# Taking PEER's gate groups of four tokens two at a time

## The chip, the cores and the metric

The kernel runs on one core of a Trainium2 chip. The metric is device time in microseconds (us) of one execution, lower is better. The kernel before takes 1953.21 us, the median of three runs (1952.89 to 1954.54).

## What is computed

Two layers of a decoder trunk on 256 tokens of width 1024. Each layer is a mixer (attention or a matrix memory) followed by PEER, a retrieval of experts; the change is in PEER. There are 128 x 128 experts. For each token and each of 8 heads the 16 best experts are found, with a softmax gate each. Then, with `u` and `v` two tables of 16384 rows:

```
act = gelu(einsum('td,thkd->thk', xb, u[ib])) * gate     # 128 chosen experts of a token
out = einsum('thk,thkd->td', act, v[ib])
```

The kernel does not gather rows. It computes gelu(u . x) for all experts, 128 tiles of 128 experts, and multiplies it by a gate matrix that is zero except at the chosen experts. For one token that gate matrix, 128 x 128, is a product of two one-hot matrices: one marks the first half of each chosen expert's number, the other marks the second half and carries the gate.

## The kernel before, in words

In one PEER stage three things run beside each other.

**The u tiles** (`h_tile`, L964). For each of the 128 tiles, SyncE loads 512 KB of `u` into `raw`. ScalarE rounds it to `hi` (L155), and VectorE writes the difference `lo` (L158). `raw`, `hi` and `lo` have three buffers each, so `hi` of a tile can be written once TensorE is through with the tile three before it. TensorE then does the products. Three tiles of four are wide: eight products of 512 columns with `hi` (L976) and eight of 256 with `lo` (L980). The fourth is narrow: 24 products of 256 columns (L181 to L183, `lo` in L183). Both come to 6144 columns. ScalarE copies half of a wide tile's result to `hs` (L984), VectorE adds the other half (L985), and gelu goes to the big array A, half by half: tokens whose gate is already in A are multiplied (ScalarE L989, VectorE L990), the others are written (ScalarE L992).

**The one-hots** (`gate_onehots`, L1101), for a group of four tokens. `oi` is made on ScalarE (four squares L1108, one relu L1109) for five groups of eight, and on VectorE (L1111) for the other three. `oj` (one buffer, L1116) and `og` (L1118) are made on VectorE. `oi` and `og` have two buffers each.

**The gate products** (`gate_group`, L1122). Eight products of 128 columns (L1131), two for each token, fill one of the two `ps_g` banks. They are then merged into A: VectorE multiplies where gelu is already there (L1139), ScalarE copies where it is not (L1141).

There are 64 groups in a layer. After an even number of u tiles the loop takes as many groups as a straight line up to tile 120 asks for. Every engine's queue is in order. A scheduler places the instructions of the whole program in these queues, by its own estimate of when their operands are there, so the order in a queue is not just that of the code. When all tiles are done, the v products (L927 to L929) begin.

Groups are counted from 0 in each layer below, and [8, 9] is the pair of groups 8 and 9.

Of the kernel before, what the change touches and what calls it, by code (L numbers as in the profile page):

```python
# [23 lines left out]
T = 256  # L24
# [11 lines left out]
G_TOK = 4  # L36
# [38 lines left out]
class Prog:  # L75
# [749 lines left out]
    def peer_body(self, layer, side, st):  # L825
# [4 lines left out]
        oh = st.enter_context(tc.tile_pool(name=f"oh{layer}", bufs=2, reuse_waits="tile"))  # L830
        hp = self.hp
        a0 = st.enter_context(tc.tile_pool(name=f"a0{layer}", bufs=1, reuse_waits="tile"))
        tabs = {"i": tab.tile([P, T], F32, name="it"), "j": tab.tile([P, T], F16, name="jt"),
                "g": tab.tile([P, 2, T], F16, name="gt")}
# [33 lines left out]
        A, i = [A0], 0  # L868
# [13 lines left out]
        a1p = tc.tile_pool(name=f"a1{layer}", bufs=1, reuse_waits="tile")  # L882
        A.append(a1p.__enter__().tile([P, 32, T, 2], F32, name="A1"))
        i_start, done = i, 0
        ohs = self.gate_onehots(oh, tabs, 0)
        while i < NEXP:
            self.h_tile(u[i], h, A, i, done, h2 if i % MERGE_OF[0] < MERGE_OF[1] else None)
            i += 1
            while done < T and i % 2 == 0 and (i == NEXP or done < T * (i - i_start) / (I_STOP - i_start)):
                nxt = self.gate_onehots(oh, tabs, done + G_TOK) if done + G_TOK < T else None  # L890
                self.gate_group(ohs, A, done, i)
                ohs = nxt
                done += G_TOK
            yield
        acc = [self.psum("acc") for _ in range(4)]
        acts = hp.tile([P, 2, 2, 4, T], F32, tag="x", name="act")
# [2 lines left out]
        for n, e in enumerate(order):  # L899
# [19 lines left out]
            if n < NEXP - 3 or n == NEXP - 1:  # L919
                if n == NEXP - 1:  # L920
                    y = [late.tile([P, D], F32, tag="raw", name="y", bufs=LATE_RING) for _ in range(TT)]
                for q in range(4):
                    half, tt = q // 2, q % 2
                    c, t = slice(512 * half, 512 * half + 512), slice(tt * P, (tt + 1) * P)
# [321 lines left out]
```

## Time and profile before

| | before |
|---|---|
| time, median of three runs | 1953.21 us |
| profiled execution | 1958.02 us |
| its span, first to last instruction | 1956.2 us |
| TensorE busy with products | 1895.7 us, 97% |
| VectorE busy | 1524.4 us, 78% |
| ScalarE busy | 1164.1 us, 60% |
| gate products | 73.1 us, 1024 products |
| mean granted TensorE clock | 0.987 |

Busy time is that of the engine as a whole; overlapping instructions count once. A row of the timeline gives an instruction's start and how long it took. Since an instruction on ScalarE or VectorE begins before the one ahead of it is fully written, the step from one start to the next is a little shorter than the duration, and it is the step that a queue pays.

### The profile page before, as it was taken

The numbers are of one execution on the slowest core, as the hardware profiler recorded it, in microseconds if no ns is written. First come the engines' busy times: TensorE is split into PE (matmuls) and PEld (weight loads), VectorE is DVE, ScalarE is ACT, GpSimd is POOL, SyncE is SP. The second block draws the span as 40 slices with busy tenths as digits, with TensorE's granted clock in tenths as the row PEclk, the third lists the DMA queues.
The fourth block names the chain that finished last, engine by engine and source line by source line (L and its number), as shares of the span: only waits on it lengthen the run. The fifth ranks groups of instructions, "written<-read, shape, count | busy, mean of one in ns | idle before, by whom it ended". The sixth has DMA issues, their size and how long they took to land.

```text
span 1956.2 us, 31712 instructions
## 1 busy us (share of the span) xinstructions
PE 1895.7 (97%) x11733; PEld 1666.4 (85%) x11733; DVE 1524.4 (78%) x3183; ACT 1164.1 (60%) x2249; POOL 40.5 (2%) x37
## 2 busy tenths in 40 slices
PE   4988999999999999999999999999999999999999
PEld 4877999989999788888877799999999988888887
DVE  8886999789998656688568889988899965556655
ACT  4664555688876544444446654568888754444443
POOL 0010000000000000000001200000000000000000
PEclk9999999999999999999989999999999999999999
DMA  8872355555555677898447343554555556669760
GB/s 326 291 255 66 122 171 189 170 164 162 170 159 177 196 216 222 301 366 294 147 150 248 119 146 117 184 183 157 168 164 167 165 172 194 194 199 358 226 197 22
DMA packets 103979, 376.24 MB, mean 192 GB/s; under 512 B 11536, under 2 KB 12944, under 8 KB 103696
## 3 DMA queue, kind: packets, MB, share of 16 engines
q1 hardware_dynamic: 103824, 374.22, 57.7%
q8 instruction: 92, 1.51, 0.3%
q14 instruction: 63, 0.52, 0.1%
HBM read 373.12 MB, written 1.05 MB: 191 GB/s over the span
## 4 chain that ended last, share of the span: by engine, by line
PE 84%; DVE 7%; issue 4%; ACT 2%; DMA 1%; POOL 1%; POOLq 0%; DVEq 0%; ACTq 0%
PE ps_h L976 13%; PE ps_acc L928 12%; PE ps_acc L929 12%; PE ps_acc L927 12%; PE ps_h L181 7%; PE ps_h L183 7%; PE ps_h L182 7%; PE ps_h L980 6%; PE ps_g L1131 3%; DVE lo L158 2%; DVE raw L248 2%; PE ps_acc L999 1%; DMA raw<-in_ev_qk_dram 1%; POOL qr L258 1%; ACT hi L155 1%
## 5 line engine op out<-in xcount | busy, mean ns | idle before, releaser
L155 ACT CAST hi<-raw 128x1024 fp32r<-128x1024 f32 x613 | 645.5, 1054 | 585.2 <-PE ps_acc L928 309.8
L158 DVE TENSOR_TENSOR lo<-raw,hi 128x1024 fp32r<-128x1024 f32 x613 | 747.9, 1221 | 303.1 <-ACT hi L155 296.0
L927 PE MATMUL ps_acc<-hi,act 128*128 128x512 f32 x1024 | 398.2, 390 | 4.4 <-ACT act L908 4.4
L928 PE MATMUL ps_acc<-hi,act 128*128 128x512 f32 x1024 | 400.5, 391 | 0.3 <-DVE act L909 0.2
L929 PE MATMUL ps_acc<-lo,act 128*128 128x512 f32 x1024 | 400.5, 391 | 0.0
L976 PE MATMUL ps_h<-h,hi 128*128 128x512 f32 x1088 | 391.1, 400 | 0.0
L181 PE MATMUL ps_h<-h,hi 128*128 128x256 f32 x1216 | 349.9, 288 | 6.9 <-ACT h L465 3.4
L183 PE MATMUL ps_h<-h,lo 128*128 128x256 f32 x1216 | 345.9, 285 | 0.5 <-DVE lo L158 0.4
L182 PE MATMUL ps_h<-h,hi 128*128 128x256 f32 x1216 | 345.4, 284 | 0.8 <-DVE h L467 0.8
L980 PE MATMUL ps_h<-h,lo 128*128 128x256 f32 x1088 | 281.4, 279 | 0.0
L181 PEld LDWEIGHTS ps_h<-h,hi 128*128 128x128 f32 x1216 | 233.9, 193 | 9.2 <-ACT h L465 4.5
L182 PEld LDWEIGHTS ps_h<-h,hi 128*128 128x128 f32 x1216 | 234.1, 193 | 3.5 <-DVE h L467 1.3
L183 PEld LDWEIGHTS ps_h<-h,lo 128*128 128x128 f32 x1216 | 233.9, 192 | 1.9 <-DVE lo L158 1.2
L976 PEld LDWEIGHTS ps_h<-h,hi 128*128 128x128 f32 x1088 | 201.0, 188 | 35.3
L927 PEld LDWEIGHTS ps_acc<-hi,act 128*128 128x128 f32 x1024 | 192.4, 188 | 44.8 <-ACT act L908 4.8
L928 PEld LDWEIGHTS ps_acc<-hi,act 128*128 128x128 f32 x1024 | 193.1, 189 | 41.2 <-DVE act L909 1.2
L929 PEld LDWEIGHTS ps_acc<-lo,act 128*128 128x128 f32 x1024 | 193.2, 189 | 40.5 <-DVE lo L158 0.7
L980 PEld LDWEIGHTS ps_h<-h,lo 128*128 128x128 f32 x1088 | 205.0, 188 | 8.5 <-DVE lo L158 0.5
L248 DVE CUSTOM_DVE_ANT_0 raw<-raw,crow,small 128x1024 f32<-128x1024 f32 x96 | 122.5, 1279 | 22.0 <-DMA raw<-in_ada_w_dram 21.9
L1108 ACT ACTIVATE oi<-iota,it 128x128 f16<-128x128 f16 x320 | 107.9, 402 | 0.0
L1118 DVE TENSOR_TENSOR og<-oj,gt 128x1024 f16<-128x1024 f16 x128 | 87.6, 684 | 3.5 <-PE ps_g L1131 2.8
L984 ACT COPY hs<-ps_h 128x256 f32<-128x256 f32 x136 | 51.1, 376 | 58.0 <-PE ps_h L976 57.8
(318 smaller groups left out, 2240.8 us busy)
## 6 DMA issues: line engine op xcount, KB each, us to landing
raw<-in_uT_dram SPq DMA_DIRECT2D x256, 512.0 KB, 3.6
raw<-in_v_dram SPq DMA_DIRECT2D x256, 512.0 KB, 4.4
raw<-in_ada_w_dram SPq DMA_DIRECT2D x96, 512.0 KB, 5.2
raw<-in_wq_dram SPq DMA_DIRECT2D x32, 512.0 KB, 4.8
raw<-in_od_qk_dram SPq DMA_DIRECT2D x16, 512.0 KB, 5.2
raw<-in_ev_in_dram SPq DMA_DIRECT2D x13, 512.0 KB, 5.4
raw<-in_ev_v_dram SPq DMA_DIRECT2D x8, 512.0 KB, 4.5
raw<-in_ev_qk_dram SPq DMA_DIRECT2D x8, 512.0 KB, 5.2
```

Of the source, the lines that this page charges most:

```text
L155: nc.scalar.copy(hi, raw)
L158: self.last_lo = nc.vector.tensor_tensor(out=lo, in0=raw, in1=hi.bitcast(F32), op=ALU.subtract)
L181: nc.tensor.matmul(ps, lhsT=whi[:, s], rhs=ahi[:, kd, :], start=kd == kds[0], stop=False)
L182: nc.tensor.matmul(ps, lhsT=whi[:, s], rhs=alo[:, kd, :], start=False, stop=False)
L183: nc.tensor.matmul(ps, lhsT=wlo[:, s], rhs=ahi[:, kd, :], start=False, stop=kd == kds[-1])
L248: nc.vector.tensor_tensor_reduce(w, w, self.crow, 1.0, self.small[:, ab:ab + 1], ALU.mult, ALU.add, m)
L927: nc.tensor.matmul(acc[q], lhsT=xhi, rhs=vhi[:, c], start=m == 0, stop=False)
L928: nc.tensor.matmul(acc[q], lhsT=xlo, rhs=vhi[:, c], start=False, stop=False)
L929: nc.tensor.matmul(acc[q], lhsT=xhi, rhs=vlo[:, c], start=False, stop=m == NEXP - 1)
L976: wide = lambda: nc.tensor.matmul(ps, lhsT=whi[:, s], rhs=both[:, kd].rearrange("p a t -> p (a t)"), start=kd == 0, stop=kd == KD - 1)
L980: nc.tensor.matmul(ps[:, :T], lhsT=wlo[:, s], rhs=both[:, kd, 0], start=False, stop=False)
L1108: nc.scalar.activation(oi[:, k, :], self.iota, AF.Square, scale=-1.0, bias=tabs["i"][:, t0 + k:t0 + k + 1])
```

## The change

```diff
-        ohs = self.gate_onehots(oh, tabs, 0)
+        pair = lambda t0: [(t, self.gate_onehots(oh, tabs, t)) for t in (t0, t0 + G_TOK)]
+        ohs = pair(0)
         while i < NEXP:
             self.h_tile(u[i], h, A, i, done, h2 if i % MERGE_OF[0] < MERGE_OF[1] else None)
             i += 1
             while done < T and i % 2 == 0 and (i == NEXP or done < T * (i - i_start) / (I_STOP - i_start)):
-                nxt = self.gate_onehots(oh, tabs, done + G_TOK) if done + G_TOK < T else None
-                self.gate_group(ohs, A, done, i)
-                ohs = nxt
-                done += G_TOK
+                for t0, o in ohs:
+                    self.gate_group(o, A, t0, i)
+                done += 2 * G_TOK
+                if done < T:
+                    ohs = pair(done)
             yield
```

Before, the one-hots of the next group were written into the second buffer ahead of the products of this group. Now both buffers hold a pair, both groups are multiplied, and then both buffers are refilled. Lines below the edit are two higher in the changed kernel (L1118 is `og` before, L1120 after).

On TensorE the 128 groups of both layers stand in 84 unbroken runs before (22 of two groups and 20 of one in each layer) and in 74 after: 27 whole pairs in each layer, and five pairs that the scheduler cut in two, with products of a u tile between the parts. Three places in the other queues follow.

VectorE, around groups 8 to 11 of the first layer, before (`lo` is the difference of a u tile, `A_1912` the half of A with the first 64 tiles, `ps_g` the gate products):

```order
L158 TENSOR_TENSOR lo<-raw,hi 128x1024
L1139 TENSOR_TENSOR A_1912<-A_1912,ps_g 128x24x8 x2
L1116 TENSOR_TENSOR oj<-iota_87,jt 128x512
L1118 TENSOR_TENSOR og<-oj,gt 128x1024
L1116 TENSOR_TENSOR oj<-iota_87,jt 128x512
L985 TENSOR_TENSOR hs<-hs,ps_h 128x256
L990 TENSOR_TENSOR A_1912<-A_1912,hs 128x36
L158 TENSOR_TENSOR lo<-raw,hi 128x1024
```

The same place after:

```order
L158 TENSOR_TENSOR lo<-raw,hi 128x1024
L992 TENSOR_TENSOR A_1912<-A_1912,hs 128x32
L992 TENSOR_TENSOR A_1912<-A_1912,gelu 128x32
L1141 TENSOR_TENSOR A_1912<-A_1912,ps_g 128x24x8 x2
L1120 TENSOR_TENSOR og<-oj,gt 128x1024
L1118 TENSOR_TENSOR oj<-iota_87,jt 128x512
L1120 TENSOR_TENSOR og<-oj,gt 128x1024
L1118 TENSOR_TENSOR oj<-iota_87,jt 128x512
L987 TENSOR_TENSOR hs<-hs,ps_h 128x256
L158 TENSOR_TENSOR lo<-raw,hi 128x1024
```

Two `og` now stand between one `lo` and the next, where one stood.

VectorE, from that `lo` to the next one, in the changed kernel (this `lo` belongs to the first u tile behind the pair [10, 11], the next to the narrow tile after it):

```order
L158 TENSOR_TENSOR lo<-raw,hi 128x1024
L992 TENSOR_TENSOR A_1912<-A_1912,hs 128x40
L987 TENSOR_TENSOR hs<-hs,ps_h 128x256
L1120 TENSOR_TENSOR og<-oj,gt 128x1024
L992 TENSOR_TENSOR A_1912<-A_1912,hs 128x40
L1141 TENSOR_TENSOR A_1912<-A_1912,ps_g 128x25x8 x2
L1113 TENSOR_TENSOR oi<-iota,it 128x512
L1118 TENSOR_TENSOR oj<-iota_87,jt 128x512
L158 TENSOR_TENSOR lo<-raw,hi 128x1024
```

Here the refill of group 13, whose `oi` is VectorE's, follows that of group 12 in one piece, ahead of the `lo`.

ScalarE, the casts of the same u tiles (`oi` one-hots, `hs` and `gelu` results of u tiles), before:

```order
L1108 ACTIVATE oi<-iota,it 128x128 x5
L1109 ACTIVATE oi<-oi 128x512
L1141 COPY A_1912<-ps_g 128x8x8
L1141 COPY A_4128<-ps_g 128x32x8
L1141 COPY A_1912<-ps_g 128x8x8
L1141 COPY A_4128<-ps_g 128x32x8
L984 COPY hs<-ps_h 128x256
L1108 ACTIVATE oi<-iota,it 128x128 x3
L989 ACTIVATE hs<-hs 128x36
L992 ACTIVATE A_1912<-hs 128x220
L1109 ACTIVATE oi<-oi 128x512
L155 CAST hi<-raw 128x1024
```

After, the second of two such stretches in a row:

```order
L991 ACTIVATE gelu<-ps_h 128x32
L994 ACTIVATE A_1912<-ps_h 128x224
L1110 ACTIVATE oi<-iota,it 128x128 x4
L1143 COPY A_1912<-ps_g 128x8x8
L1143 COPY A_4128<-ps_g 128x32x8
L1143 COPY A_1912<-ps_g 128x8x8
L1143 COPY A_4128<-ps_g 128x32x8
L1111 ACTIVATE oi<-oi 128x512
L1110 ACTIVATE oi<-iota,it 128x128 x4
L986 COPY hs<-ps_h 128x256
L1111 ACTIVATE oi<-oi 128x512
L155 CAST hi<-raw 128x1024
```

Both stretches hold two whole `oi` ahead of one cast `hi`. The order of SyncE's transfers does not change, nor does any engine's order outside the two gate stretches.

## Rows read from the trace of the kernel before

**Rows 1.** The page, part 1: busy time, share of the span, instructions.

```profile
PE 1895.7 (97%) x11733; PEld 1666.4 (85%) x11733; DVE 1524.4 (78%) x3183; ACT 1164.1 (60%) x2249; POOL 40.5 (2%) x37
```

**Rows 2.** Windows: length, each engine's busy time (x instructions), granted clock, DMA share, GB/s.

```profile
358.50:621.00 262.50, 262.50 (x1994) 237.86 (x1993) 236.09 (x477) 215.50 (x581) 0.00 (x0) 1.00 0.52 163
1310.80:1573.40 262.60, 262.60 (x1994) 237.94 (x1994) 236.63 (x477) 215.48 (x581) 0.00 (x0) 1.00 0.51 164
...
648.00:650.00 2.00, 2.00 (x6) 1.54 (x6) 1.33 (x2) 0.00 (x0) 0.00 (x0) 0.50 0.56 203
```

**Rows 3.** Chain that ended last, 390 to 420 us, share by line.

```profile
by line: PE ps_h L976 45.1%; PE ps_h L980 22.6%; PE ps_g L1131 12.4%; PE ps_h L181 6.8%; PE ps_h L182 6.7%; PE ps_h L183 6.7%
```

**Rows 4.** Timeline of TensorE: start, us, engine, line, tiles, count.

```profile
409.69 1.08 PE L1131 MATMUL ps_g<-oi,og 128*128 128x128 f16 x16
410.59 0.47 PE L976 MATMUL ps_h<-h,hi 128*128 128x512 f32 x1
410.90 0.28 PE L980 MATMUL ps_h<-h,lo 128*128 128x256 f32 x1
411.02 0.40 PE L976 MATMUL ps_h<-h,hi 128*128 128x512 f32 x1
411.25 0.28 PE L980 MATMUL ps_h<-h,lo 128*128 128x256 f32 x1
...
413.45 0.28 PE L181 MATMUL ps_h<-h,hi 128*128 128x256 f32 x1
413.57 0.28 PE L182 MATMUL ps_h<-h,hi 128*128 128x256 f32 x1
```

**Rows 5.** Waits, first gate stretch: who waited for whom, total, times, longest.

```profile
ACT hi L155 <- DMA raw<-in_uT_dram: 1.3, 3, 0.9
...
PEld ps_h L980 <- DVE lo L158: 0.2, 1, 0.2
```

**Rows 6.** Timeline of ScalarE.

```profile
391.53 1.56 ACT L1108 ACTIVATE oi<-iota,it 128x128 f16<-128x128 f16 x5
392.99 0.62 ACT L1109 ACTIVATE oi<-oi 128x512 f16<-128x512 f16 x1
393.51 0.86 ACT L1141 COPY A<-ps_g 128x64 f32<-128x64 f32 x4
394.23 0.41 ACT L984 COPY hs<-ps_h 128x256 f32<-128x256 f32 x1
394.50 1.03 ACT L1108 ACTIVATE oi<-iota,it 128x128 f16<-128x128 f16 x3
395.39 0.26 ACT L989 ACTIVATE hs<-hs 128x36 f32<-128x36 f32 x1
...
396.31 1.07 ACT L155 CAST hi<-raw 128x1024 fp32r<-128x1024 f32 x1
397.25 0.40 ACT L984 COPY hs<-ps_h 128x256 f32<-128x256 f32 x1
```

**Rows 7.** Timeline of VectorE; the last field is idle time before.

```profile
398.55 0.42 DVE L985 TENSOR_TENSOR hs<-hs,ps_h 128x256 f32<-128x256 f32 x1
398.88 0.69 DVE L1118 TENSOR_TENSOR og<-oj,gt 128x1024 f16<-128x1024 f16 x1
399.49 0.19 DVE L990 TENSOR_TENSOR A<-A,hs 128x36 f32<-128x36 f32 x1
399.59 0.63 DVE L1139 TENSOR_TENSOR A<-A,ps_g 128x200 f32<-128x200 f32 x2
400.14 0.42 DVE L1116 TENSOR_TENSOR oj<-iota,jt 128x512 f16<-128x512 f16 x1
...
402.90 1.22 DVE L158 TENSOR_TENSOR lo<-raw,hi 128x1024 fp32r<-128x1024 f32 x1 [0.77 <-ACT hi L155]
...
404.55 0.68 DVE L1111 TENSOR_TENSOR oi<-iota,it 128x512 f16<-128x512 f16 x1
405.16 1.21 DVE L158 TENSOR_TENSOR lo<-raw,hi 128x1024 fp32r<-128x1024 f32 x1
```

## The prediction

> **What bounds the kernel now.** I read the page's busy times first: TensorE is busy 97% of the span, no other engine above 78% [rows 1]. Then windows, because only two stretches matter, from the first gate product to the last in each layer. There TensorE is busy for the whole of both, 262.50 of 262.50 us and 262.60 of 262.60, at granted clock 1.00 [rows 2]. VectorE is close behind, 236.09 us (90%), ScalarE at 215.50 (82%). The chain that ended last consists in this stretch of TensorE's products alone [rows 3]: nothing else ends a wait that counts. The waits say the same: TensorE's only wait for a partner is one of 0.2 us for a `lo` [rows 5]. So the reader should see a stage in which the bound engine is already full. The edit can take little from it; it can put waits into it.
>
> **What sixteen products in a row give.** The products are the same 1024. Sixteen in a row already occur: they start at 409.69 and the next u product at 410.59, so 0.90 us, 56 ns each [rows 4]. What a run costs beside its products is at its end: the first wide product to its `lo` product takes 0.31 us behind the run (410.59 to 410.90) and 0.23 later (411.02 to 411.25), so at most 0.08 us a run. Five fewer runs in a layer (42 to 37) give back 0.4 us. If the one `lo` wait of 0.2 us goes too, a layer gains 0.6 us at most.
>
> **What the later refill costs.** Nothing is added to VectorE's or ScalarE's work; its order changes. Before, a group's one-hots were written while the other buffer was in use. Now both refills come in one piece behind the pair, and whatever stands behind them in the in-order queues comes later: `hi` on ScalarE, `lo` on VectorE, which TensorE needs for its next tiles. Steps, start to start: square 0.29 (five in 1.46), relu 0.52, four gate copies 0.72, `hs` copy with three squares 1.16, a gelu pair 0.40 (0.92 from gelu to cast, less a relu), cast 0.94 [rows 6]; `hs` add 0.33, `og` 0.61, the short multiply of A 0.10, two gate multiplies 0.55, VectorE's `oi` 0.61 [rows 7]. For `oj` and the last `lo` I take whole durations, 0.42 and 1.22. A u tile takes 2.86 us (410.59 to 413.45) [rows 4]; a narrow tile has as many columns, so it is given the same.
>
> I lay these along the changed order at its tightest place, with 0 at the end of the pair [6, 7]. TensorE's order is: a wide and a narrow tile to 5.72, pair [8, 9] to 6.62, two wide tiles to 12.34, [10, 11] to 13.24, a wide tile to 16.10, a narrow one, two wide ones, [12, 13].
> - ScalarE ends an earlier cast at about 0.3 (it waits for the tile ahead of [6, 7], 0.9 before 0, then copies `hs` and casts). The next stretch, with both `oi` of [8, 9], is 0.40 + 1.46 + 0.72 + 0.52 + 1.16 + 0.52 + 0.94 = 5.72, so to 6.0. Its second relu is done at 5.1, before the pair needs it at 5.72.
> - The stretch behind it holds [10, 11]: two gelu pairs 0.80, eight squares 2.34, copies 0.72, two relus 1.04, `hs` 0.27, cast 0.94, together 6.11. So that cast ends at 12.15 and its relu at 11.2, again ahead of 12.34.
> - VectorE writes that tile's `lo` to 13.37. TensorE starts the tile at 13.24 and wants `lo` 0.23 later: it just fits.
> - To the next `lo` VectorE has 0.10 + 0.33 + 0.61 + 0.10 + 0.55 + 0.61 + 0.42 + 1.22 = 3.94, so to 17.31. The narrow tile starts at 16.10 and wants `lo` with its third product, 0.24 later (a step of 0.12 each [rows 4]), at 16.34. **TensorE waits 0.97 us.**
>
> Behind that no pair stands for four tiles, and the lead comes back. The same working at [16, 17] gives a cast at 18.94 and a `lo` at 20.16 where TensorE wants it at 19.86, since the scheduler has put twelve gate products ahead of it: 0.30 us. At four other meetings that I followed (before [4, 5], and at [26] to [32], [42] to [44], [50] to [52]) the `lo` or relu comes 0.2 to 1.0 us early. That is within the error of such a sum, so no wait is counted there, but the range must know it.
>
> The ring of three `raw` buffers is freed by the same `lo`, so a late `lo` also sends a load late; ScalarE waited for these loads 1.3 us in the whole stretch [rows 5] and the casts lead, so this is costed at 0. If that cover goes, the longest such wait, 0.9 us, is what one place could cost.
>
> Both `ps_g` banks are now filled together. The copies out of them end on ScalarE at 0.3 + 0.40 + 1.46 + 0.72 = 2.9, and the next pair wants the banks at 5.72. So the rows make this free. The Trainium skill's "Perfetto Trace Analysis" (section Optimizing Tensor Performance, Matmuls) says that independent groups should rotate through PSUM banks, so that emptying one overlaps with products into the next. Filling both and emptying both goes against it: by that rule alone up to 2.9 us a pair would be bare, 186 us in the 64 pairs of both layers. Here the emptying lies beside two u tiles, and no row shows it bare, so I stay with 0.
>
> **The sum.** A layer: 0.97 + 0.30 - 0.2 - 0.4 = +0.67 us. Two layers: +1.3. The profiled execution of 1958.02 would become 1959.3. It stands 4.8 us above the median of the runs; the difference is carried over: 1953.2 + 1.3 = 1954.5 us. Ends: no new wait at all, -1.2, so 1952.0; each of the seven meetings of two ScalarE-made pairs in a layer paid in full, below.
>
> **Rivals.**
> - *Every meeting pays (slower).* Five of eight groups have `oi` on ScalarE, so pairs 0, 2 and 8, 10 and so on follow each other with two full `oi` each; seven of eight such meetings in a layer come two tiles apart. If each costs what I found at one, 7 x 0.97 x 2 = 13.6, less 0.8 for the runs: 1966.0 us. For it: spares of 0.2 to 1.0 on a chain of 12 us; steps 5% longer than the rows, 0.6 us, would turn most into waits. Against: it decides only if VectorE is late at several of them, and in between, wherever a pair is skipped for two tiles, the lead returns. TensorE full before and VectorE at 90% speak for both.
> - *The pair waits for its own one-hots (slower still).* With nothing written ahead, the refill has 5.72 us where pairs come two tiles apart. My relus and `og` are 0.6 to 1.1 us early. If they were late by 0.5 us at each of some 22 such pairs, 22 x 0.5 x 2 = 22: 1975 us. Against it: the scheduler put u products ahead of five pairs in each layer, so TensorE has work there. The Trainium skill's "Perfetto Trace Analysis" (section Optimization Strategy) says the same gap repeating on the engine that should be full can mean too few buffers; this would be that gap. The trace of before has no such gap, and no row shows the new one.
> - *Nothing happens.* The scheduler has fitted the order, all spares hold: 1952.0 to 1953.2 us.
> - *Faster.* It would need more than the 1.2 us that the stretches can give. The one other place is behind each stretch, where the clock falls to 0.50 (1.2 GHz) at the start of the v products [rows 2]. Were that spared, about 1.7 us a layer would come back: 1953.2 - 1.2 - 3.4 = 1948.6 us. But the wait that precedes it comes from the last u tile's gelu, whose order is unchanged.
>
> **Chances.** My forecast with its own small errors (up to some 2 us of waits in a layer) 0.44, nothing happens 0.19, every meeting pays or most do 0.25, the pair waits 0.08, faster 0.04. A measurement of this kernel can tell 0.2%, 3.9 us, from no change: 1949.3 to 1957.1 counts as the same. The forecast and "nothing" lie within it, 0.63, of which I give 0.01 to faster; slower is 0.33, faster 0.05, same 0.62. The range goes from 1952.0, the bound without waits, to 1964, which takes in the every-meeting case as far as most meetings pay; what it leaves out is about 0.05 below and 0.15 above.
>
> **What would show it.** Right: both gate stretches still 262 to 264 us long; TensorE's waits for `lo` rise from one of 0.2 us to a few, the longest about 1 us, at the narrow tile behind [10, 11] and at the wide tile with [18] in it; the clock stays 1.00 there. Every-meeting rival: seven waits of about 1 us per stretch. Pair rival: waits of gate products for `oi` or `og`. Wrong: a stretch shorter than 261.5 us, or a difference outside of the two stretches.

## The result, and the profile after

The changed kernel took **1965.2 us** (median of 3 runs, 1964.2 to 1966.3) against 1953.2 us. The ratio on record is 1.0054 with the interval [1.0041, 1.0068]; it is not the quotient of the two medians, which is 1.0061. It is slower, and by more than the 0.2% that I had named as what a measurement of this kernel can tell. I had forecast 1954.5 us and a range up to 1964.0. The median lies 1.2 us above the range; by the ratio the time would be 1963.8, just inside. Either way the forecast of 1.3 us more was 9 us or more short, and the likeliest case was not the one that came. Five more runs of the same kernel, beside the experiments below, gave 1964.5 us and 1.0055 [1.0042, 1.0069].

Its profiled execution took 1966.3 us with a span of 1964.5. The page's first part, as in [rows 1] (lines of `peer_body` and below stand two further down than before: 976 is now 978, 980 is 982, 1131 is 1133):

```profile
PE 1900.6 (97%) x11733; PEld 1667.4 (85%) x11733; DVE 1528.0 (78%) x3181; ACT 1164.4 (59%) x2245; POOL 40.5 (2%) x37
```

By these shares nothing has happened. The windows of the two gate stretches, as in [rows 2], and of two microseconds behind the first one, say more: the first number behind the window is its length, then come TensorE's products, its weight loads, VectorE, ScalarE, and, behind GpSimd's 0.00, the granted clock.

```profile
358.89:619.76 260.87, 258.83 (x1954) 232.89 (x1953) 232.51 (x468) 212.07 (x573) 0.00 (x0) 1.00 0.50 160
1315.04:1576.18 261.14, 258.99 (x1954) 232.92 (x1953) 232.42 (x468) 211.90 (x573) 0.00 (x0) 1.00 0.50 160
652.00:654.00 2.00, 2.00 (x6) 1.60 (x5) 1.46 (x2) 0.00 (x0) 0.00 (x0) 0.50 0.60 176
```

TensorE was busy for the whole of both stretches in [rows 2]; now it stands idle for 2.0 and 2.2 us of them. The windows are not shorter work done faster: the last pair of groups comes two tiles earlier than the last group did, 1954 products lie between first and last instead of 1994. The clock is 1.00 in the stretches and falls to 0.50 (1.2 GHz) behind them, both as before.

Idle time alone undercounts, since a product that starts late is also recorded as longer (0.38 us for 0.28 in the rows further down). So I add up **gaps**: the time from each product's start to the next one's, less a fixed step for its kind, near the usual one (0.230 us wide, 0.123 for its `lo` product, 0.118 narrow, 0.056 gate product), over a gate stretch. Before: 2.02 and 2.00 us in the two layers. After: 6.09 and 6.36. That is 8.4 us more, and from the first wide tile to the last the layers took 4.3 and 4.6 us longer. The waits of the first stretch show who was late. The columns are who waited for whom, total, times, longest; of TensorE's waits for another engine only those of weight loads (`PEld`) are shown here, and those of 0.3 us in all and less are left out:

```profile
DVE lo L158 <- ACT hi L155: 21.1, 26, 2.3
ACT hi L155 <- DMA raw<-in_uT_dram: 5.4, 10, 1.6
PEld ps_h L982 <- DVE lo L158: 1.4, 3, 0.7
PEld ps_h L183 <- DVE lo L158: 1.1, 2, 1.0
PEld ps_h L978 <- ACT A L994: 0.5, 1, 0.5
PEld ps_h L978 <- DVE hs L987: 0.4, 1, 0.4
PEld L1133 <- DVE og L1120: 0.4, 1, 0.4
```

In [rows 5] one 0.2 us for a `lo` stood here; the trace of before has two more of 0.2 us there, of weight loads of gate products (L1131). Most of it is `lo`; the gate products' own wait for a one-hot (`og`) is 0.4. Loads come later too (ScalarE waits 5.4 us for them instead of 1.3), but no wait of TensorE for a cast stands among these rows.

Seven gaps over 0.15 us, 3.45 us together, make up most of layer 0's loss (before there was one, 0.18). Layer 1 has the same seven, within 0.04, and one more of 0.32:

| at, us | place | gap, us | predicted |
|---|---|---|---|
| 398.45 | first wide tile behind [10, 11], `lo` | 0.43 | 0 ("just fits") |
| 401.89 | narrow tile behind it, `lo` | 0.92 | 0.97 |
| 432.05 | wide tile with [18] and half of [19] in it, `lo` | 0.22 | 0.30 |
| 483.26 | behind [30, 31], bank of `ps_h` not emptied | 0.42 | not looked at |
| 512.88 | between [38] and [39], `hs`; `og` | 0.42 + 0.38 | not looked at |
| 514.39 | behind [39], `lo` | 0.66 | not looked at |

The first place, as the chain of waits from 397 to 403.5 us has it (start, us, engine, tile, line):

```profile
396.86 0.94 ACT hi L155
397.80 0.02 issue
397.83 1.22 DVE lo L158
399.05 0.11 DVE A L992
399.16 0.33 DVE hs L987
399.49 0.60 DVE og L1120
400.09 0.12 DVE A L992
400.21 0.59 DVE A L1141 x2
400.80 0.60 DVE oi L1113
401.40 0.33 DVE oj L1118
401.73 1.15 DVE lo L158
402.88 0.04 issue
402.93 0.38 PE ps_h L183
```

In [rows 3] the chain was TensorE's products alone. Here it runs through VectorE, and in the order that the prediction laid out: from one `lo` to the next 3.83 us (399.05 to 402.88), predicted 3.94. TensorE's rows around it:

```profile
398.45 0.47 PE L978 MATMUL ps_h<-h,hi 128*128 128x512 f32 x1
399.11 0.38 PE L982 MATMUL ps_h<-h,lo 128*128 128x256 f32 x1 [0.18 <-DVE lo L158]
...
401.89 0.28 PE L182 MATMUL ps_h<-h,hi 128*128 128x256 f32 x1
402.93 0.38 PE L183 MATMUL ps_h<-h,lo 128*128 128x256 f32 x1 [0.76 <-DVE lo L158]
```

The reader should take the start of the next row, not the bracket: from 401.89 to 402.93 it is 1.04 us for a step of 0.12.

The dearest place is another one, which the prediction did not look at. From the chain from 510 to 516 us:

```profile
510.75 0.60 DVE oi L1113
511.35 0.60 DVE og L1120
511.96 0.60 DVE oi L1113
512.56 0.34 DVE oj L1118
512.89 0.41 DVE hs L987
513.31 0.60 DVE og L1120
513.91 1.15 DVE lo L158
515.06 0.04 issue
515.10 0.39 PE ps_h L982
```

Groups 38 and 39 both have their `oi` on VectorE. It writes `oi`, `og`, `oi` and `oj` in a row ahead of the `hs` that frees a bank of `ps_h`, and then the second `og` ahead of the `lo`; `hs`, `og` and `lo` all come late. On TensorE:

```profile
512.46 0.64 PE L1133 MATMUL ps_g<-oi,og 128*128 128x128 f16 x8
513.36 0.49 PE L978 MATMUL ps_h<-h,hi 128*128 128x512 f32 x1 [0.26 <-DVE hs L987]
513.97 0.64 PE L1133 MATMUL ps_g<-oi,og 128*128 128x128 f16 x8
515.10 0.39 PE L982 MATMUL ps_h<-h,lo 128*128 128x256 f32 x1 [0.49 <-DVE lo L158]
```

Here the sixteen products don't even stand in a row: a wide product is between the two groups.

### The profile page after: what moved, and what is told of

The parts are those of the page before. It is cut to its first block, busy times and chain, and to the rows that moved or that the text cites. A ratio compares the mean times of both kernels' runs of the same rounds, so it can differ in the third digit from the quotient of the medians.

```text
span 1964.5 us, 31732 instructions
## 1 busy us (share of the span) xinstructions
PE 1900.6 (97%) x11733; PEld 1667.4 (85%) x11733; DVE 1528.0 (78%) x3181; ACT 1164.4 (59%) x2245; POOL 40.5 (2%) x37
## 4 chain that ended last, share of the span: by engine, by line
PE 76%; DVE 11%; ACT 6%; issue 5%; DMA 1%; POOL 1%; POOLq 0%; DVEq 0%; ACTq 0%
PE ps_acc L931 12%; PE ps_acc L930 12%; PE ps_acc L929 12%; PE ps_h L978 11%; PE ps_h L982 6%; PE ps_h L181 5%; PE ps_h L183 5%; PE ps_h L182 5%; DVE lo L158 4%; PE ps_g L1133 2%; DVE raw L248 1%; ACT hi L155 1%; ACT oi L1110 1%; POOL qr L258 1%; DMA raw<-in_ada_w_dram 1%
## 5 line engine op out<-in xcount | busy, mean ns | idle before, releaser
L1120 DVE TENSOR_TENSOR og<-oj,gt 128x1024 f16<-128x1024 f16 x128 | 87.6, 684 | 0.6
```

## The experiments

The theory after the result: the refill of two groups is a lump of work for VectorE and ScalarE that now has to be done between two pairs. Where two pairs stand two tiles apart and a lump falls on one engine, `lo` or a bank of `ps_h` comes late. Rivals: both PSUM banks filled together, or sixteen products in a row, cost by themselves; asking for the one-hots behind the products instead of ahead is what costs, whether one group or two; the loss lies outside of the stretches. The last two columns are from all runs; the gaps are of the profiled one.

| kernel | gaps, layer 0 + 1, us | median, us | ratio to before [95%] |
|---|---|---|---|
| before, first profile | 2.02 + 2.00 | 1953.2 | |
| before, again | 2.04 + 2.02 | 1953.8 | 1.0003 [0.9993, 1.0013] |
| changed, first profile | 6.09 + 6.36 | 1965.2 | 1.0054 [1.0041, 1.0068] |
| changed, again | 5.86 + 5.98 | 1964.5 | 1.0055 [1.0042, 1.0069] |
| two at a time, no refill | 1.43 + 1.27 | 1951.8 | 0.9988 [0.9979, 0.9997] |
| one at a time, no refill | 1.64 + 1.71 | 1951.2 | 0.9985 [0.9975, 0.9995] |
| one at a time, refill behind | 4.62 + 4.59 | 1958.0 | 1.0022 [1.0013, 1.0031] |
| two at a time, asked ahead | 4.19 + 3.83 | 1956.4 | 1.0016 [1.0007, 1.0025] |
| two, refill in two parts | 5.41 + 6.15 | 1961.7 | 1.0040 [1.0027, 1.0054] |
| two, mixed pairs | 3.22 + 3.21 | 1953.4 | 1.0005 [0.9995, 1.0014] |
| two, every pair mixed | 3.75 + 3.75 | 1957.4 | 1.0020 [1.0009, 1.0030] |
| two, more meetings | 11.19 + 13.26 | 1974.8 | 1.0112 [1.0097, 1.0128] |
| two, asked ahead, mixed | 2.61 + 2.58 | 1957.5 | 1.0015 [1.0007, 1.0024] |
| before, mixed | 1.67 + 1.64 | 1953.4 | 0.9995 [0.9985, 1.0005] |

**No refill behind the pairs.**

```diff
-                if done < T:
-                    ohs = pair(done)
+                ohs = [(t0 + 2 * G_TOK, o) for t0, o in ohs]
```

> The changed kernel in which the one-hots are written for the first two groups only, and all other groups multiply with these: ScalarE's squares and relus and VectorE's oj, og and oi of 62 groups a layer are left out, while all 1024 gate products, their copies and multiplies stay at the same tiles. If the refill in the in-order queues makes lo late, the gaps fall below 1 us a layer: 1965 less 2 x 5.5 = 1954 us or somewhat less. If the two banks filled together, their copies or the pace cost, the gaps stay near 6 us a layer and the time at 1963 to 1966 us.

The gaps fall to 1.4 and 1.3 us a layer, less than before if not under the 1 us expected, and the time is 2.3 us (0.6 to 4.1) under the kernel before. Sixteen products in a row, both banks filled together, and all copies and multiplies of A are still there. TensorE's waits in its first stretch, all that are listed for its products and loads:

```profile
PEld L1132 <- issue: 2.7, 17, 0.2
```

No `lo`, no `hs`, no `og`; the kernel before has as much of this row (3.0 us, 19 times). So the waits need the refill; the two banks alone cost nothing. This kernel takes the refill's work away as well as its place, so it cannot tell which of the two makes the waits; the kernels with a refill below move only its place.

**One group at a time, no refill.**

```diff
-        ohs = self.gate_onehots(oh, tabs, 0)
+        two = [self.gate_onehots(oh, tabs, t) for t in (0, G_TOK)]
...
-                nxt = self.gate_onehots(oh, tabs, done + G_TOK) if done + G_TOK < T else None
-                self.gate_group(ohs, A, done, i)
-                ohs = nxt
+                self.gate_group(two[done // G_TOK % 2], A, done, i)
```

> One group at a time at the tiles of the kernel before, the one-hots written for the first two groups only and used for all (the refills of 62 groups a layer are left out). Against the pairs without refills it differs by nothing but the runs of gate products: if a run costs 0.08 us, as I took it, the pairs' fewer runs are worth 0.4 us a layer and this one has gaps of 1.7 to 1.8 us a layer for their 1.4; the time is 0.8 us more, about 1952.6 us. If sixteen products in a row give more than that, the distance is 2 us or more.

Gaps of 1.68 a layer on the mean, where the pairs have 1.35: taking two at a time is worth 0.33 us a layer when nothing has to be refilled. In time the two cannot be told apart, their intervals overlap.

**Which half of the change costs.** The change does two things: it takes groups two at a time, and it asks for one-hots behind the products instead of ahead. One kernel for each alone. The first has the old pace, with both buffers full from the start and each asked for again behind its own products; the second takes pairs but asks for the next group's one-hots ahead of each group:

```diff
# one at a time, refill behind
+        ohs = [self.gate_onehots(oh, tabs, t) for t in (0, G_TOK)]
...
+                self.gate_group(ohs.pop(0), A, done, i)
+                if done + 2 * G_TOK < T:
+                    ohs.append(self.gate_onehots(oh, tabs, done + 2 * G_TOK))
+                done += G_TOK
# two at a time, asked ahead
+                for _ in range(2):
+                    nxt = self.gate_onehots(oh, tabs, done + G_TOK) if done + G_TOK < T else None
+                    self.gate_group(ohs, A, done, i)
+                    ohs = nxt
+                    done += G_TOK
```

> One group at a time again, as in the kernel before, but with the changed kernel's refill: both buffers are full at the start, and each is written again only behind the eight products that used it. If taking two groups in a row is what costs (one refill of both buffers stands as one piece in the queues), this runs as the kernel before: 1953 us, both gate stretches 262.5 to 263 us, TensorE's gaps in them near 2 us a layer. If it is the loss of the order 'next one-hots ahead of this group's products' that costs, it runs as the changed kernel: 1962 to 1966 us, gaps near 6 us a layer. I expect 1953 to 1957.

> Sixteen products in a row as in the changed kernel, at the same tiles, but the one-hots are asked for as in the kernel before: those of the next group ahead of the products of this one. If the bunching of the work (two groups' copies, multiplies and refills between the same two tiles) is what costs, this is as slow as the changed kernel, 1963 to 1967 us, with waits for lo at the same narrow tile behind [10, 11]. If the order of asking is what costs, it is at 1953 to 1956 us. I expect 1960 to 1966, since the second group's buffer still comes free with the first one's.

Both expectations were of the all-or-nothing kind, and both missed. Gaps a layer, the mean of two: 2.0 (one, ahead), 4.6 (one, behind), 4.0 (two, ahead), 5.9 (two, behind, second profile). Each half costs 2 us or more alone, and together 3.9, not quite the sum. What the asking moves is seen in VectorE's order: asked behind the products, a refill stands in the code before the `u` tiles that follow, asked ahead of the next products it stands behind them. From the `oj` of group 7 to that of group 8, VectorE has `oj`, `lo`, `hs`, `og`, A, `lo`, `oj` in the kernel before and `oj`, `lo`, `og`, `hs`, `oj` with the refill behind (A and the next `lo` come later): `og` has gone ahead of `hs`, and an `oj` ahead of a `lo`, which TensorE needs first. No large gap lies at this place, but one does behind [13] (0.54 us, TensorE's `lo` product at 410.43): there VectorE has `oj`, `hs`, `oi`, `og`, A, `oj` between one `lo` (405.10) and the next (409.15), where the kernel before has one `og` between the same two (405.16 and 406.89). With the pairs asked ahead TensorE's waits move from `lo` to the one-hots of the second group: its largest gaps (0.16 to 0.30 us, six a layer) lie in or beside runs of gate products. Of its waits for other engines in the first stretch, each 0.2 us, those of gate products are

```profile
PEld L1132 <- DVE oj L1117: 0.2, 1, 0.2
PEld L1132 <- DVE lo L158: 0.2, 1, 0.2
PEld L1132 <- DVE og L1119: 0.2, 1, 0.2
```

**The refill in two parts**, the second buffer asked for behind the next `u` tile:

```diff
             i += 1
+            for t in owed:
+                ohs.append((t, self.gate_onehots(oh, tabs, t)))
+            owed = []
...
-                    ohs = pair(done)
+                    ohs = [(done, self.gate_onehots(oh, tabs, done))]
+                    owed = [done + G_TOK]
```

> The changed kernel, but only the first buffer is asked for behind the pair; the second one's refill is asked for behind the next u tile. Sixteen products in a row and both PSUM banks as before, the same engines for the same oi. If the piece of two refills in the queues is the cause, the two halves with a tile's work between them cost less: gaps of 3 to 4 us a layer, 1956 to 1959 us. If ScalarE's sum of work from pair to pair is the cause, wherever it stands, nothing is gained: 1962 to 1966 us.

It gains little: 11.6 us of gaps for 11.8, 7.8 us (5.3 to 10.5) above the kernel before. That speaks against the piece as such. What has to be done between two pairs is the same, and here it delays other things: there are five waits for a wide tile's `lo` instead of three, and gate products wait for ScalarE's `oi`, behind [40] for 0.33 us in layer 0 and 1.30 in layer 1. Without that one long wait the gain would be some 1 us.

**Who writes `oi`.** Three kernels leave the order of asking as the change has it and deal out the `oi` differently:

```diff
-        if self.ngate % 8 < J_ACT:
+        if self.ngate % 8 in (0, 2, 4, 6, 7):   # mixed pairs
+        if self.ngate % 2 == 0:                 # every pair mixed
+        if self.ngate % 16 < 2 * J_ACT:         # more meetings
```

> The changed kernel with the same number of oi on ScalarE and on VectorE (five and three of eight), but dealt out so that three pairs of four have one of each, and no two pairs with both on ScalarE follow each other. If the waits come from meetings of two pairs whose oi are both ScalarE's, as my sum and the rival of every meeting have it, most of the seven or eight waits a layer go: gaps from some 6 to 2 or 3 us a layer, 1956 to 1959 us. If sixteen products in a row or the two PSUM banks filled together cost by themselves, nothing moves: 1965 us.

> The changed kernel with every second oi on ScalarE, so that each pair has one of each engine and no meeting is left. VectorE gets one more oi in eight groups, 8 x 0.61 = 4.9 us more in a stretch where it is busy for some 236 of 262. If the meetings are the cause, the gaps are 2 to 3 us a layer and the time 1952 to 1955 us, at or just under the kernel before. If VectorE is what runs out, it is 1956 to 1962 us.

> The changed kernel with the same five of eight oi on ScalarE, dealt out in sixteens: the first ten groups, five pairs, on ScalarE and the next six, three pairs, on VectorE. Pairs with both oi on ScalarE now follow each other four times in 16 groups, 16 times a layer where it was 8. If these meetings are the cause, at some 0.5 us each, the gaps go from 6 to about 10 or 11 us a layer and the time to 1971 to 1976 us. If it is the refill in one piece whoever writes it, or sixteen products in a row, nothing moves: 1962 to 1966 us.

Mixed pairs, with as many `oi` on each engine as before, have 5.4 to 6.0 us fewer gaps than the changed kernel, and their time is that of the kernel before within the interval (+1.0 us, -1.0 to +2.7), less than the 1956 to 1959 us expected. Of the changed kernel's seven large gaps a layer none is left at its place; there are three new ones around groups 52 and 53, 1.40 us together, with VectorE late by `hs`, `og` and `lo` in turn. The first stretch:

```profile
PEld ps_h L183 <- DVE lo L158: 0.7, 1, 0.7
PEld L1133 <- DVE og L1120: 0.4, 1, 0.4
PEld ps_h L978 <- DVE hs L987: 0.4, 1, 0.4
PEld ps_h L982 <- DVE lo L158: 0.2, 1, 0.2
```

With every pair mixed VectorE has one `oi` more in eight groups. The gaps rise to 3.75: the same three, and 0.56 us between groups 62 and 63, for a `lo`. Removing every pair whose two `oi` are ScalarE's did not bring the expected 1952 to 1955 us; VectorE is what is short there, as the rival of that expectation had it.

Dealt out so that like pairs follow like, the gaps double, and the time is 21.9 us (18.9 to 25.0) above the kernel before. Its first stretch has

```profile
PEld ps_h L982 <- DVE lo L158: 2.7, 6, 1.1
PEld ps_h L183 <- DVE lo L158: 2.3, 3, 1.1
PEld ps_h L978 <- DVE hs L987: 1.1, 2, 0.6
PEld L1133 <- DVE og L1120: 1.0, 3, 0.4
```

So who writes the two `oi` of a pair decides most of the cost. These three kernels don't separate ScalarE's pairs from VectorE's: mixed pairs leave no pair to VectorE alone and one of four instead of two to ScalarE alone ([6, 7] of every eight), and the last kernel adds meetings of both.

**The two best together, and the dealing in the kernel before.** The edit is the mixed pairs' line in the pairs asked ahead, and in the kernel before.

> Pairs with the kernel before's look-ahead (8.0 us of gaps in both layers) and the mixed dealing of oi (6.4 us with the changed kernel's order). If the two remedies work on the same waits, nothing is added: gaps of 6 to 8 us, 1955 to 1957 us. If they work on different ones, gaps of 3 to 4 us: 1952 to 1953 us, the best of the pairs.

> The kernel before, one group at a time with its look-ahead, and the oi dealt out as in the mixed pairs (groups 0, 2, 4, 6, 7 of eight on ScalarE). Its gaps are 2.0 us a layer, those without any refill 1.4: if dealing out helps here too, at most 1.2 us in all are to be had, 1952 us. If its order needs the runs of five, it loses some: 1954 to 1956 us. I expect no difference that can be told.

In the gaps the two remedies add up in part: alone they take some 4 and some 6 us off the changed kernel's 12, together 7, which leaves 5.2 us in both layers, between the two cases expected. It is the least of all pairs with a refill, though still above the kernel before. In time the first shows none of that (+2.9 us, 1.4 to 4.7). The kernel before, dealt out mixed, loses its one wait for a `lo`, 0.7 us of gaps in all, which no measurement here can tell (1.0 us less, from 2.9 less to 1.0 more). No version that writes all its one-hots was found that is faster than the kernel before by what can be measured.

**The same kernels again.**

> The changed kernel itself, once more and beside the variants. The gaps of TensorE in the two gate stretches of its first profile are 8.4 us longer than in the kernel before, its time of three runs 12.0 us above the median before. If the stretches are the whole of the loss, more runs bring the difference to 8 or 9 us: 1961 to 1963. If something outside of them is lost too, it stays near 12: 1965.

> The kernel before once more, with a profile of its own: its first profiled execution was 1958.0 us, 4.8 above the median. If that excess lies outside of the gate stretches, this one shows the same 2.0 us of gaps in each and a shorter rest: 1953 us. If the stretches themselves differ from run to run, the gaps come out otherwise.

The kernel before has the same gaps, 4.06 us, in a span of 1950.1 us instead of 1956.2: what its first profiled run had more lies outside of the gate stretches. The changed kernel's difference stays near 10.7 us (8.2 to 13.5), while its gaps are 7.8 to 8.4 us longer and its two layers, from first wide tile to last, 8.3 to 8.9. The interval takes that in, but some 2 us may be lost elsewhere; the pairs asked ahead with mixed dealing have a like surplus of time over gaps (+2.9 us, 1.4 to 4.7, for 1.1). The profiles can't tell: outside of these two spans they have 1386.6 and 1380.4 us before and 1385.9 and 1385.2 after, so the kernel before alone differs by 6 us. Where a surplus lies, if there is one, was not found.

## Why the prediction was wrong

- **The bound: right.** The stage had little to give and something to lose. The sixteen products in a row give 0.33 us a layer when nothing is refilled, predicted 0.4; the old wait for a `lo` was 0.2.
- **The mechanism: right.** VectorE's queue delays `lo` behind the lump, at the narrow tile behind [10, 11], by 0.92 us (predicted 0.97), and at the tile with [18] by 0.22 (0.30). Nothing changed in the clock, and no wait of TensorE for the copies out of the two `ps_g` banks is seen.
- **The step that failed is the list of places.** I followed the meetings of pairs whose `oi` are ScalarE's, found two that pay, and wrote of four others that their spare of 0.2 to 1.0 us "is within the error of such a sum, so no wait is counted there". At three of the four there is no gap over 0.15 us; the stretch from [26] ends at the one behind [30, 31], which is for a bank and neither for `lo` nor for a relu. And of the 3.45 us in the table 2.3 lie at places where I counted nothing: the wide tile that "just fits" (0.43), the bank behind [30, 31] (0.42) and pair [38, 39], both of VectorE (1.46). I had priced VectorE's `oi` at 0.61 us, but the working lays no pair with two of them along the order, though VectorE at 90% [rows 2] was the side engine with the least to spare. The gap behind [30, 31] is of another kind: the gelu that empties the bank stands on ScalarE behind a cast, and this cast (482.45) had itself waited 0.52 us for TensorE.
- **"Just fits" was a wait.** With the end of [10, 11] at 13.24 of that working, 398.45 us, the cast ended at 12.59 instead of 12.15 and its `lo` at 13.84 instead of 13.37. TensorE, wanting it 0.31 us behind the run, paid 0.35 of it. The term that was wrong is the start of ScalarE's chain, not its steps. ScalarE's rows at [6, 7], whose products start at 384.39:

```profile
384.64 0.37 ACT L986 COPY hs<-ps_h 128x256 f32<-128x256 f32 x1 [0.71 <-PE ps_h L978]
384.90 1.06 ACT L155 CAST hi<-raw 128x1024 fp32r<-128x1024 f32 x1
385.86 0.22 ACT L991 ACTIVATE hs<-hs 128x24 f32<-128x24 f32 x1
...
391.60 0.25 ACT L991 ACTIVATE hs<-hs 128x32 f32<-128x32 f32 x1
```

  The sum lets the `hs` copy start with the first gate product; it started 0.25 us later, so the earlier cast was done at 385.86, which is 0.65 of the working and not 0.3. The two stretches behind took 5.74 and 6.20 us for 5.72 and 6.11. A place that fits by nothing is better entered with a part of the sum's error than with 0: where it comes late TensorE pays, where it comes early TensorE gains nothing.
- **The rest is small.** The gaps over 0.15 us, 7.2 us in both layers against 0.35 before, are 6.8 of the 8.4 us; the other 1.6 are steps below 0.15 us each.
- **The rival "every meeting pays" came out at the right time, 1966.0 us, in good part by luck.** There are seven gaps in layer 0 and eight in layer 1, where it said seven, but they sum to 3.45 us and not to seven times 0.97, and four of the seven are not at meetings of ScalarE's pairs. Its own test, mixed pairs, took most of the loss away, and doubled meetings doubled it; but these kernels move VectorE's pairs as well.
- **The rival "the pair waits for its own one-hots"** is seen at one place a layer, [38, 39], where 0.38 us is a wait for `og`; I had it at some 22.
- **One sign misled.** I had named a stretch shorter than 261.5 us as a sign of being wrong. Both stretches came out shorter, 260.87 and 261.14 us, in a kernel that is slower: the last pair comes two tiles earlier than the last group did, which I had not counted.
- **The Trainium skill's two rules.** The Trainium skill's "Perfetto Trace Analysis" (section Optimizing Tensor Performance, Matmuls) has independent groups rotate through PSUM banks, and by that rule alone 186 us would have been bare. Both banks are filled together in the pairs without refill too, and their gaps are 1.35 us a layer, less than one group at a time: the trace does not bear that price out; other products stand between the pairs. That page's rule that the same gap repeating can mean too few buffers (section Optimization Strategy) fits what is seen only in part: the gaps come at seven places, not at every pair. More one-hot buffers were not tried.

## What to carry to other kernels

When an edit lumps the side engines' work together, lay the longest lump of each engine along the order, not only that of the engine you suspect: here the dearest place, 1.46 us, was that of the engine already at 90%. At a bound engine that is full, enter a place with a spare near 0 as a wait in the sum, since nothing early elsewhere paid it back here. And before undoing such an edit look at who writes what: dealing the same work out more evenly, so that VectorE never had two `oi` in one lump and ScalarE's double lumps never met, brought back most of what the edit cost.

## What the runs showed that was not expected

- In the changed kernel and the kernel before, the gaps repeat while the times don't: 0.42, 0.38 and 0.66 us at groups 38 and 39, within 0.01 us, in both layers and both profiles of the changed kernel, and 4.02 and 4.06 us in all in two profiles of the kernel before whose spans are 6.1 us apart. Here adding up one stage's steps told more than the times of whole runs. It is not so in every kernel: with more meetings the two layers of one profile have 11.19 and 13.26 us, and the 1.30 us of the refill in two parts stands in one layer only.
- A run of gate products costs less at its end than its first step shows. I read at most 0.08 us a run from [rows 4]; one group at a time and two at a time without refill have 41 and 31 such ends a layer and differ by 0.33 us, 0.03 a run.
- Asking for the same one-hots behind the eight products instead of ahead of them costs 2.6 us of gaps a layer at the old pace, though the one-hots are then asked for sooner: at the two places that were looked at they go ahead of `hs` or `lo` in VectorE's queue, and TensorE needs these first.
